# Pair sums and down-projection sums on VectorE instead of GpSimd, in the first and last feed-forward pair and the first down group

## The chip, the core and the metric

The kernel runs on one core of one Trainium2 chip. The metric is the device time of one execution in microseconds (us). Three runs of the kernel before gave 1433.92 to 1436.02 us, with a median of 1434.41 us. The engines are called here as the profile calls them: PE (TensorE matmul), DVE (VectorE), ACT (ScalarE), POOL (GpSimd) and SP (SyncE, whose queue issues the DMAs).

## What is computed

One layer of a decoder, for 1024 tokens of width 1024. The change touches the feed-forward part alone:

```
x = x + concat([y_nsa, y_conv, y_gla]) @ w_out
h = rms_norm(x, ffn_norm_g)
x = x + (silu(h @ ffn_w_gate) * (h @ ffn_w_up)) @ ffn_w_down     # D_FF = 2816
```

All arrays are float32. Ahead of it stand the token mixers and the output projection, behind it a gated per-layer embedding and a last norm.

## The kernel before

**Precision.** Each float32 operand of a product is split in two: `split` (L1037) copies it to the reduced format on ACT (L1039, the high part) and has the rest subtracted on DVE (`sub`, L267, the low part). A product then takes three matmuls: high by high, high by low, low by high. So a matmul waits for ACT where it reads a high part and for DVE where it reads a low part.

**Fewer products.** Gate and up projection run over eleven column groups c of 256. For each c there is one `Pair` for gate (n = 0) and one for up (n = 1). A `Pair` loads two weight tiles `nat` (row blocks m and m+1) and cuts them into four quarters a11, a12, a21, a22. Seven products of quarter sums stand in for eight of quarters (a scheme of the Strassen and Winograd kind). `first` and `second` multiply a11 and a12; `sums` makes s = a21+a22 and then s-a11; `fifth` and `sixth` multiply these; `sixth` also makes a11-a21 and a12-s; `rest` multiplies these and a22, and adds earlier results to later ones (p6+p1, p67+p1). `quarters` puts the four output quarters together and scales them by the norm's factor `rbc1`. For up, the quarters are then multiplied with silu(gate), two of the four (`UPP`) on POOL. On the other side, `Right.make` forms sums of the activations h once (t1 to t4, four tiles each) ahead of the first pair.

In the kernel before, the sums of `Pair.sums`, `sixth` and `rest`, one sum in `quarters`, the two `UPP` products and the sum t3 run on POOL: per c 16 instructions of 128x512 with both inputs in SBUF.

**Down.** The activations of each c go to DRAM (`actd`) as sums; `Down` loads them and two tiles of `w_d` again for groups of up to three c (`DOWN`), and `operands` makes the weight sums: for product 5 b12-b11, for product 6 b22 minus that, for product 7 b22-b12, for product 4 b21 minus the sum. All are on POOL. `drain` adds finished banks into x on DVE (L1335).

**Order.** Two things set it. A dry pass over the code (`_Recorder`) estimates when each tile is last used, with a price per element and engine (`COST`; a `tensor_tensor` on POOL 2.2, on DVE 0.95), and gives each tile one of 50 slots in SBUF; so a tile's load must wait until the tile that had its slot is done. Then the framework puts the instructions of each engine, and the DMAs of SP's queue, in an order by a simulated timeline. Each engine keeps to its order: one that waits holds up all behind it. The last pair (c = 10) and the first down group overlap: `Down` loads and sums stand among the pair's last products.

Of the kernel before, what the change touches and what calls it, by code (L numbers as in the profile page):

```python
# [13 lines left out]
ALU = mybir.AluOpType  # L14
# [12 lines left out]
MF = FF // P  # L27
# [65 lines left out]
UPP = (1, 3)  # L93
PT = 5
PATH = "vvvp"
DOWN = ((0, 1, 2), (3, 4, 5), (6, 7, 8), (9, 10))
# [122 lines left out]
def tile_block(ctx: ExitStack, tc: tile.TileContext, a: dict, out: bass.AP, plan: Plan):  # L219
    nc = tc.nc  # L220
# [27 lines left out]
    class Ring:  # L248


        def __init__(self, lo, hi):
            self.lo, self.hi, self.at = lo, hi, lo
# [13 lines left out]
    def sub(eng, o, i0, i1):  # L266
        return eng.tensor_tensor(out=o, in0=i0, in1=i1, op=ALU.subtract)  # L267
# [449 lines left out]
    for t in range(NT):  # L717
# [11 lines left out]
        if t > 2:  # L729
            pump(near, 1)  # L730
    nc.vector.tensor_tensor(out=gcmp, in0=gates.rearrange("p t (h b) -> p t h b", b=3)[:, :, :, 0],
                            in1=rowok.unsqueeze(2).to_broadcast([P, NT, H]), op=ALU.mult)
# [41 lines left out]
    for which in range(2):  # L774
# [4 lines left out]
        for u in range(2):  # L779
            for g in range(2):  # L780
                src = cv[g * 64:(g + 1) * 64, :].rearrange("p (n j) -> p j n", j=16)
                for q in range(2):
                    js = slice(q * 8, q * 8 + 8)
                    nc.vector.tensor_tensor(
                        out=X[q][u * 64:(u + 1) * 64, :, g * NCMP:(g + 1) * NCMP],
                        in0=src[:, js, u:u + NCMP],
                        in1=pos[g * 64:(g + 1) * 64, u, js].unsqueeze(2).to_broadcast([64, 8, NCMP]), op=ALU.add)
# [249 lines left out]
    def split(src):  # L1037
        o = B("op", F32R, (P, 2, 512))
        nc.scalar.copy(o[:, 0, :], src)  # L1039
        sub(nc.gpsimd if pool_lo[0] > 0 else nc.vector, o[:, 1, :], src, f(o[:, 0, :]))  # L1040
        pool_lo[0] -= 1
        return o

    def half(x, n):
        return x[:, n * 512:(n + 1) * 512]
# [8 lines left out]
    class Right:  # L1054
# [6 lines left out]
        def make(self, *names):  # L1061
            for k, (l, u) in enumerate(zip(self.lower, self.upper)):
                b11, b12 = half(l, 0), half(l, 1)
                b21, b22 = (half(u, 0), half(u, 1)) if u is not None else (None, None)
                for n in names:
                    if n == "t1":
                        sub(nc.vector, b11, b12, b11)
                    if n == "t2":
                        sub(nc.vector, b11, b22, b11)
                    if n == "t3":  # L1070
                        sub(nc.gpsimd, b12, b22, b12)
                    if n == "t4":
                        sub(nc.vector, b11, b21, b11)
                    self.x[n][k] = split({"21": b21, "22": b22, "t3": b12}.get(n, b11))

    class Pair:


        def __init__(self, src, m, right):
            w = []  # L1080
            for i in (m, m + 1):
                w.append(B("nat"))
                nc.sync.dma_start(out=w[-1], in_=src[i])
            self.a11, self.a12, self.a21, self.a22 = (half(w[q // 2], q % 2) for q in range(4))
            self.x, self.b, self.c, self.w5 = right.x, None, None, None

        def first(self, second=True):
            cp = B("cp", F32, (P, 2, 512))
# [10 lines left out]
        def sums(self):  # L1099
            ws = B("ws", F32, (P, 2, 512))  # L1100
            self.s, self.s3 = ws[:, 0, :], ws[:, 1, :]
            nc.gpsimd.tensor_tensor(out=self.s, in0=self.a21, in1=self.a22, op=ALU.add)
            self.w5 = split(self.s)
            sub(nc.gpsimd, self.s, self.s, self.a11)

        def fifth(self):
            if self.w5 is None:
# [7 lines left out]
        def sixth(self):  # L1115
            if self.w5 is None:
                self.sums()
            w6 = split(self.s)
            sub(nc.gpsimd, self.s3, self.a11, self.a21)
            sub(nc.gpsimd, self.s, self.a12, self.s)  # L1120
            self.b = bank()
            prod(w6, self.x["t2"], self.b, True, False)
            nc.scalar.copy(self.p6, self.b)  # L1123

        def rest(self):
            if self.b is None:
                self.sixth()
            s, s3 = self.s, self.s3
            if self.c is None:
                self.fifth()  # L1130
            prod(split(s3), self.x["t3"], self.b, False, False)
            nc.scalar.copy(self.p67, self.b)
            nc.gpsimd.tensor_tensor(out=self.p6, in0=self.p6, in1=self.p1, op=ALU.add)
            nc.gpsimd.tensor_tensor(out=self.p67, in0=self.p67, in1=self.p1, op=ALU.add)
            prod(split(s), self.x["22"], self.c, False, True)
            prod(split(self.a22), self.x["t4"], self.b, False, True)

# [126 lines left out]
    def quarters(p, out):  # L1264

        rr = half(rbc1, 0), half(rbc1, 1)
        add = lambda eng, o, i0, i1: eng.tensor_tensor(out=o, in0=i0, in1=i1, op=ALU.add)
        mult = lambda eng, o, i0, i1: eng.tensor_tensor(out=o, in0=i0, in1=i1, op=ALU.mult)
        c11, c12, c21, c22 = out
        mult(nc.vector, c11, p.a, rr[0])  # L1270
        add(nc.vector, c12, p.c, p.p6)
        mult(nc.vector, c12, c12, rr[1])
        add(nc.vector, c21, p.b, p.p1)
        mult(nc.vector, c21, c21, rr[0])
        add(nc.gpsimd, c22, p.p67, p.p5)
        mult(nc.vector, c22, c22, rr[1])

    for c in range(MF // 2):
        if c == MF // 2 - 1:
            for n in range(2):  # L1280
                pairs[c, n] = Pair(a["w_u" if n else "w_g"], 2 * c, r)
                pairs[c, n].first()
            for n in range(2):
                pairs[c, n].sixth()
            for n in range(2):
                pairs[c, n].fifth()
        for n in range(2):
            if (c, n) not in pairs:
                pairs[c, n] = Pair(a["w_u" if n else "w_g"], 2 * c, r)
                pairs[c, n].first()  # L1290
            p = pairs.pop((c, n))
            p.rest()
            if n == 0:
                act = [B("sg") for _ in range(2)]
                quarters(p, [half(g, i) for g in act for i in range(2)])
                for g in act:
                    nc.scalar.activation(g, g, AF.Silu)
            else:
                up_ = [B("ws", F32, (P, 512)), p.p6, p.p1, p.p5]
                quarters(p, up_)  # L1300
                for i, o in enumerate(up_):
                    g = half(act[i // 2], i % 2)
                    (nc.gpsimd if i in UPP else nc.vector).tensor_tensor(out=g, in0=o, in1=g, op=ALU.mult)

                a11, a21, a12, a22 = (half(g, i) for g in act for i in range(2))
                sa = B("sa", F32, (P, 2, 512))
                s5, s6, s3 = sa[:, 0, :], sa[:, 1, :], up_[0]
                nc.vector.tensor_tensor(out=s5, in0=a21, in1=a22, op=ALU.add)
                sub(nc.vector, s6, s5, a11)
                sub(nc.vector, s3, a12, s6)  # L1310
                sub(nc.vector, a21, a11, a21)
                nc.sync.dma_start(out=actd[c, 0:2].rearrange("i p j -> p i j"), in_=sa)
                nc.sync.dma_start(out=actd[c, 2], in_=s3)
                nc.sync.dma_start(out=actd[c, 3:5].rearrange("i p j -> p i j"), in_=act[0].rearrange("p (i j) -> p i j", i=2))
                nc.sync.dma_start(out=actd[c, 5], in_=a22)
                nc.sync.dma_start(out=actd[c, 6], in_=a12)
# [17 lines left out]
    def add(o, i0, eng=nc.vector):  # L1334
        eng.tensor_tensor(out=o, in0=i0, in1=o, op=ALU.add)  # L1335

    class Down:


        def __init__(self, c):  # L1340
            self.c, self.a = c, {}
            w = []
            for m in (2 * c, 2 * c + 1):
                w.append(B("nat"))
                nc.sync.dma_start(out=w[-1], in_=a["w_d"][m * P:(m + 1) * P, :])
            self.b11, self.b12, self.b21, self.b22 = (half(x, i) for x in w for i in range(2))
            self.load(5, 6)
            st = B("st", F32, (P, 2, 512))
            self.t, self.a[2] = st[:, 0, :], st[:, 1, :]
            nc.sync.dma_start(out=self.a[2], in_=actd[c, 6])  # L1350
# [7 lines left out]
        def operands(self, n):  # L1358
            x = self
            if n == 5:  # L1360
                x.load(3, 1)
                sub(nc.gpsimd, x.t, x.b12, x.b11)
            if n == 6:
                sub(nc.gpsimd, x.t, x.b22, x.t)
            if n == 3:
                x.load(7, 4)
            if n == 7:
                sub(nc.gpsimd, x.b12, x.b22, x.b12)
            if n == 4:
                sub(nc.gpsimd, x.t, x.b21, x.t)  # L1370
            return split(x.a.pop(n)), split({3: x.b22, 1: x.b11, 7: x.b12, 2: x.b21}.get(n, x.t))
# [30 lines left out]
    for q, cs in enumerate(DOWN):  # L1402
        ds = [Down(c) for c in cs]
        for n, g, start in ((5, 0, True), (6, 1, True), (3, 0, False), (1, 0, True), (7, 1, False), (4, 1, False),
# [17 lines left out]
            for t in range(4):  # L1422
                c = slice(t * P, (t + 1) * P)
# [26 lines left out]
    for i, t in enumerate(ORDER):  # L1450
        c = slice(t * P, (t + 1) * P)
        x, r3 = rows[i]
# [128 lines left out]
```

## Time and profile before

| | |
|---|---|
| median of three runs | 1434.41 us (1433.92 to 1436.02) |
| profiled execution | 1426.49 us, of which its span 1424.7 us |
| PE busy | 1380.7 us, 97% |
| DVE busy | 1034.4 us, 73% |
| POOL busy | 692.8 us, 49% |
| ACT busy | 662.6 us, 47% |
| mean granted PE clock | 0.993 |

The profile is of one execution, so durations and waits are read from it and set against its 1426.49 us. A stretch is given in us from the start of the span. The output projection ends at 636 us, the feed-forward pairs fill 636 to about 1081 us, and the first down group begins at 1076 us among the last pair's products. A PE row in brackets tells how long PE stood idle before an instruction and what ended the wait. POOL spans are rough.

### The profile page before, as it was taken

The numbers are of one execution on the slowest core, as the hardware profiler recorded it, in microseconds if no ns is written. First come the engines' busy times: TensorE is split into PE (matmuls) and PEld (weight loads), VectorE is DVE, ScalarE is ACT, GpSimd is POOL, SyncE is SP. The second block draws the span as 40 slices with busy tenths as digits, with TensorE's granted clock in tenths as the row PEclk, the third lists the DMA queues.
The fourth block names the chain that finished last, engine by engine and source line by source line (L and its number), as shares of the span: only waits on it lengthen the run. The fifth ranks groups of instructions, "written<-read, shape, count | busy, mean of one in ns | idle before, by whom it ended". The sixth has DMA issues, their size and how long they took to land.

```text
span 1424.7 us, 19476 instructions
## 1 busy us (share of the span) xinstructions
PE 1380.7 (97%) x7080; PEld 1159.6 (81%) x7080; DVE 1034.4 (73%) x1782; ACT 662.6 (47%) x1290; POOL 692.8 (49%) x680
## 2 busy tenths in 40 slices
PE   8999999999999989999899999999998999999997
PEld 6898777889999978887788877877786878887886
DVE  3897548468999885658767767676788998887533
ACT  7321522257888884545433333333334444444532
POOL 3751433438887872045566555655485514303111
PEclk9999999999999999999999999999999999999999
DMA  9201012500000023521232331233365733521111
GB/s 361 68 16 40 25 53 86 167 1 5 9 5 5 5 79 119 188 79 45 100 109 95 110 108 63 83 110 111 141 235 205 258 132 127 171 81 63 68 41 45
DMA packets 55743, 135.68 MB, mean 95 GB/s; under 512 B 5412, under 2 KB 10206, under 8 KB 55646
## 3 DMA queue, kind: packets, MB, share of 16 engines
q1 hardware_dynamic: 55502, 134.42, 27.1%
q8 instruction: 55, 0.90, 0.3%
q14 instruction: 42, 0.34, 0.1%
q10 hardware_dynamic: 144, 0.01, 0.0%
HBM read 102.68 MB, written 31.73 MB: 94 GB/s over the span
## 4 chain that ended last, share of the span: by engine, by line
PE 58%; DVE 16%; POOL 9%; ACT 6%; issue 6%; DMA 4%; SPq 0%; POOLq 0%; DVEq 0%; ACTq 0%
DVE op L267 8%; PE banks L1426 7%; POOL ws L267 4%; PE banks L966 3%; PE banks L371 3%; PE banks L372 3%; PE banks L368 3%; ACT op L1039 3%; PE banks L1010 2%; PE banks L1011 2%; PE banks L906 2%; PE banks L1476 2%; PE banks L1477 2%; PE banks L1478 2%; PE banks L907 2%
## 5 line engine op out<-in xcount | busy, mean ns | idle before, releaser
L1050 PE MATMUL banks<-op 128*128 128x512 f32 x616 | 238.8, 394 | 4.7 <-ACT cp L1123 3.0
L1052 PE MATMUL banks<-op 128*128 128x512 f32 x616 | 239.8, 392 | 3.0 <-DVE op L267 3.0
L1051 PE MATMUL banks<-op 128*128 128x512 f32 x616 | 240.7, 391 | 0.7 <-DVE op L267 0.7
L1426 PE MATMUL banks<-op 128*128 128x512 f32 x924 | 214.8, 394 | 8.4 <-DVE op L267 4.6
L1426 PEld LDWEIGHTS banks<-op 128*128 128x128 f32 x924 | 174.8, 190 | 48.0 <-DVE op L267 6.5
L1039 ACT CAST op<-nat 128x512 fp32r<-128x512 f32 x200 | 117.7, 619 | 174.3 <-DVE op L267 64.0
L267 DVE TENSOR_TENSOR op<-nat,op 128x512 fp32r<-128x512 f32 x196 | 164.9, 864 | 38.5 <-ACT op L1039 37.9
L267 DVE TENSOR_TENSOR op<-ws,op 128x512 fp32r<-128x512 f32 x88 | 99.5, 1131 | 73.4 <-ACT op L1039 69.6
L1050 PEld LDWEIGHTS banks<-op 128*128 128x128 f32 x616 | 115.9, 188 | 36.6 <-ACT cp L1123 8.9
L1052 PEld LDWEIGHTS banks<-op 128*128 128x128 f32 x616 | 116.0, 188 | 28.8 <-DVE op L267 3.9
L1051 PEld LDWEIGHTS banks<-op 128*128 128x128 f32 x616 | 116.1, 188 | 24.7 <-DVE op L267 1.1
L921 POOL TENSOR_SCALAR p<-p,sums,gates 128x640 f32<-128x640 f32 (+7 forms) x128 | 100.4, 795 | 36.4 <-DVE sums L917 26.8
L1039 ACT CAST op<-ws 128x512 fp32r<-128x512 f32 x88 | 54.0, 623 | 105.1 <-POOL ws L267 65.1
L912 ACT ACTIVATE p<-p,mn 128x640 f32<-128x640 f32 (+7 forms) x128 | 94.7, 742 | 10.2 <-DVE mn L909 10.1
L368 PE MATMUL banks<-hT,whi 128*128 128x512 f32 x208 | 83.9, 404 | 6.8 <-ACT hT L324 6.3
L371 PE MATMUL banks<-hT,whi 128*128 128x512 f32 x208 | 83.4, 401 | 0.5 <-DVE hT L325 0.5
L372 PE MATMUL banks<-hT,wlo 128*128 128x512 f32 x208 | 82.1, 396 | 0.0
L966 PE MATMUL banks<-cst,p 128*128 128x128 f32 x448 | 71.2, 274 | 2.3 <-DVE pt L267 1.3
L906 PE MATMUL banks<-k,qst 128*128 128x512 f32 (+2 forms) x192 | 68.0, 360 | 1.0 <-POOL qst L267 0.5
L267 DVE TENSOR_TENSOR pt<-banks,pt 128x512 fp32r<-128x512 f32 (+1 forms) x114 | 64.1, 570 | 6.1 <-ACT pt L977 5.2
L1335 DVE TENSOR_TENSOR x<-banks,x 128x512 f32<-128x512 f32 x96 | 63.4, 679 | 5.5 <-PE banks L1426 5.4
L267 POOL TENSOR_TENSOR st<-nat 128x512 f32<-128x512 f32 x11 | 21.1, 1919 | 90.7 <-DMA nat<-in_w_d 84.2
(299 smaller groups left out, 3402.0 us busy)
## 6 DMA issues: line engine op xcount, KB each, us to landing
nat<-actd SPq DMA_DIRECT2D x33, 512.0 KB, 5.6
nat<-in_w_g SPq DMA_DIRECT2D x22, 512.0 KB, 3.2
nat<-in_w_u SPq DMA_DIRECT2D x22, 512.0 KB, 4.0
nat<-in_w_d SPq DMA_DIRECT2D x22, 512.0 KB, 6.2
nat<-in_w_t SPq DMA_DIRECT2D x13, 512.0 KB, 4.2
actd<-sg SPq DMA_DIRECT2D x22, 256.0 KB, 2.2
actd<-sa SPq DMA_DIRECT2D x11, 512.0 KB, 5.3
actd<-sg SPq DMA_DIRECT2D x11, 512.0 KB, 5.3
```

What stands on the lines that cost most here:

```text
L267: return eng.tensor_tensor(out=o, in0=i0, in1=i1, op=ALU.subtract)
L368: r = mm(o, hi[:, w], x[:, 0, :], start=kt == 0, stop=False)
L371: mm(o, hi[:, w], x[:, 1, :], start=False, stop=False)
L372: mm(o, lo_[:, w], x[:, 0, :], start=False, stop=kt == KT - 1)
L906: mark("pe", mm(ps[:, :max(w, 256)], q, kdup[br][g][:, k], start=True, stop=False))
L921: nc.gpsimd.tensor_scalar(out=ps_out[br][:, :n], in0=ps_out[br][:, :n], scalar1=sums[:, br:br + 1], scalar2=gates[:, qb, 3 * head(h) + 1 + ...
L966: nc.tensor.transpose(ps[:, (2 * m + e) * P:(2 * m + e + 1) * P], blk(e, kb, br, ka), ident)
L1039: nc.scalar.copy(o[:, 0, :], src)
L1050: mm(ps, w[:, 0, c], x[k][:, 0, :], start=start and k == 0, stop=False, skip_group_check=True)
L1051: mm(ps, w[:, 0, c], x[k][:, 1, :], start=False, stop=False, skip_group_check=True)
L1052: mm(ps, w[:, 1, c], x[k][:, 0, :], start=False, stop=k == 3, skip_group_check=True)
L1426: mm(groups[g][t], r[:, v, c], l[:, u, :], start=start and (i, u, v) == (0, 0, 0), stop=i == len(ops) - 1 and u == 1, skip_group_check=True)
```

## The change

`Pair` and `Down` get an attribute `eng`. It is DVE for the pairs of c = 0 and c = 10 (m = 0 and MF-2) and for the down products of the first group (c = 0, 1, 2), and POOL elsewhere. The sums named above use it; of `Down.operands`, those for products 5 and 6, while those for 7 and 4 stay on POOL. The four sums t3 go to DVE too. Per `Pair` that is seven instructions, for up two more: 4 x 7 + 2 x 2 = 32, with t3 36, with 3 x 2 of `Down` 42 instructions, all 128x512 float32 with both inputs in SBUF.

```
                     if n == "t3":
-                        sub(nc.gpsimd, b12, b22, b12)
+                        sub(nc.vector, b12, b22, b12)
...
             self.x, self.b, self.c, self.w5 = right.x, None, None, None
+
+            self.eng = nc.vector if m in (0, MF - 2) else nc.gpsimd
...
-            nc.gpsimd.tensor_tensor(out=self.s, in0=self.a21, in1=self.a22, op=ALU.add)
+            self.eng.tensor_tensor(out=self.s, in0=self.a21, in1=self.a22, op=ALU.add)
             self.w5 = split(self.s)
-            sub(nc.gpsimd, self.s, self.s, self.a11)
+            sub(self.eng, self.s, self.s, self.a11)
...
-            sub(nc.gpsimd, self.s3, self.a11, self.a21)
-            sub(nc.gpsimd, self.s, self.a12, self.s)
+            sub(self.eng, self.s3, self.a11, self.a21)
+            sub(self.eng, self.s, self.a12, self.s)
...
-            nc.gpsimd.tensor_tensor(out=self.p6, in0=self.p6, in1=self.p1, op=ALU.add)
-            nc.gpsimd.tensor_tensor(out=self.p67, in0=self.p67, in1=self.p1, op=ALU.add)
+            self.eng.tensor_tensor(out=self.p6, in0=self.p6, in1=self.p1, op=ALU.add)
+            self.eng.tensor_tensor(out=self.p67, in0=self.p67, in1=self.p1, op=ALU.add)
...
-        add(nc.gpsimd, c22, p.p67, p.p5)
+        add(p.eng, c22, p.p67, p.p5)
...
-                    (nc.gpsimd if i in UPP else nc.vector).tensor_tensor(out=g, in0=o, in1=g, op=ALU.mult)
+                    (p.eng if i in UPP else nc.vector).tensor_tensor(out=g, in0=o, in1=g, op=ALU.mult)
...
             self.c, self.a = c, {}
+            self.eng = nc.vector if c in DOWN[0] else nc.gpsimd
...
-                sub(nc.gpsimd, x.t, x.b12, x.b11)
+                sub(x.eng, x.t, x.b12, x.b11)
...
-                sub(nc.gpsimd, x.t, x.b22, x.t)
+                sub(x.eng, x.t, x.b22, x.t)
```

The order of the engines' instructions moves with it. Three places matter here.

First SP's queue at the second column group. `nat_6896` and `nat_6898` are the first and second weight tile of its up pair (c = 1, n = 1); the `sg` and `sa` rows are stores of the first column group's activations. Before:

```order
L1083 DMA nat_6763<-in_w_g 128x1024
L1083 DMA nat_6765<-in_w_g 128x1024
L1083 DMA nat_6898<-in_w_u 128x1024
L1315 DMA actd_2366<-sg_6665 128x512
L1083 DMA nat_6896<-in_w_u 128x1024
L1312 DMA actd_2366<-sa_6753 128x2x512
```

The same place of the changed kernel:

```order
L1083 DMA nat_6763<-in_w_g 128x1024
L1083 DMA nat_6765<-in_w_g 128x1024
L1083 DMA nat_6896<-in_w_u 128x1024
L1317 DMA actd_2366<-sg_6665 128x512
L1318 DMA actd_2366<-sg_6665 128x512
L1083 DMA nat_6898<-in_w_u 128x1024
L1314 DMA actd_2366<-sa_6753 128x2x512
```

The first tile stood behind a store and now stands ahead of it; the second stands behind two stores.

Next DVE where the last pair (`ws_9352`, `cp_9260`, `cp_9296`) meets the first down group (`st_9539` and `st_9547` are weight sums, the `op` rows low parts). Before:

```order
L1268 TENSOR_TENSOR ws_9511<-banks_67,rbc1_6583 128x512
L267 TENSOR_TENSOR op_9358<-ws_9352,op_9358 128x512
L267 TENSOR_TENSOR op_9563<-st_9539,op_9563 128x512
L267 TENSOR_TENSOR op_9481<-ws_9352,op_9481 128x512
L267 TENSOR_TENSOR op_9560<-nat_9537,op_9560 128x512
L267 TENSOR_TENSOR op_9496<-nat_9294,op_9496 128x512
L267 TENSOR_TENSOR op_9572<-st_9547,op_9572 128x512
```

Of the changed kernel:

```order
L1270 TENSOR_TENSOR ws_9511<-banks_67,rbc1_6583 128x512
L267 TENSOR_TENSOR st_9539<-nat_9533 128x512
L1270 TENSOR_TENSOR sg_9452<-banks_67,rbc1_6583 128x512
L267 TENSOR_TENSOR op_9358<-ws_9352,op_9358 128x512
L1135 TENSOR_TENSOR cp_9260<-cp_9260 128x512
L267 TENSOR_TENSOR ws_9352<-nat_9292,ws_9352 128x512
L267 TENSOR_TENSOR op_9563<-st_9539,op_9563 128x512
L267 TENSOR_TENSOR op_9560<-nat_9537,op_9560 128x512
L267 TENSOR_TENSOR st_9539<-nat_9535,st_9539 128x512
L267 TENSOR_TENSOR op_9481<-ws_9352,op_9481 128x512
L267 TENSOR_TENSOR op_9496<-nat_9294,op_9496 128x512
L267 TENSOR_TENSOR st_9547<-nat_9541 128x512
```

The sums now stand among the low parts; three of them read weight tiles of the down group (`nat_9533`, `nat_9535`, `nat_9541`) that SP's queue loads at this place.

Last POOL at the same place. Before:

```order
L267 TENSOR_TENSOR st_9547<-nat_9541 128x512
L267 TENSOR_TENSOR nat_9541<-nat_9543,nat_9541 128x512
L1133 TENSOR_TENSOR cp_9296<-cp_9296 128x512
L267 TENSOR_TENSOR st_9547<-nat_9543,st_9547 128x512
L1134 TENSOR_TENSOR cp_9376<-cp_9376,cp_9260 128x512
L1267 TENSOR_TENSOR sg_9453<-cp_9376 128x512
L267 TENSOR_TENSOR st_9555<-nat_9549 128x512
```

Of the changed kernel:

```order
L267 TENSOR_TENSOR nat_9533<-nat_9535,nat_9533 128x512
L267 TENSOR_TENSOR nat_9541<-nat_9543,nat_9541 128x512
L267 TENSOR_TENSOR nat_9549<-nat_9551,nat_9549 128x512
L267 TENSOR_TENSOR st_9539<-nat_9535,st_9539 128x512
L267 TENSOR_TENSOR st_9547<-nat_9543,st_9547 128x512
L267 TENSOR_TENSOR st_9555<-nat_9551,st_9555 128x512
```

Only the six sums for products 7 and 4 are left on POOL there.

## Rows read from the trace of the kernel before

**Rows 1.** The page's part 1: busy us, share of span, instructions.

```profile
PE 1380.7 (97%) x7080; PEld 1159.6 (81%) x7080; DVE 1034.4 (73%) x1782; ACT 662.6 (47%) x1290; POOL 692.8 (49%) x680
```

**Rows 2.** Seven stretches: length, busy us (instructions) of PE, PEld, DVE, ACT, POOL, PE clock, DMA.

```profile
625.00:664.00 39.00, 38.30 (x177) 31.45 (x176) 35.48 (x43) 24.49 (x42) 19.48 (x16) 1.00 0.11 41
664.00:700.00 36.00, 31.23 (x126) 24.02 (x125) 28.00 (x30) 13.28 (x22) 28.06 (x25) 0.96 0.27 95
690.00:700.00 10.00, 5.91 (x19) 4.12 (x18) 7.93 (x9) 2.73 (x5) 6.08 (x4) 0.85 0.54 202
1050.00:1092.00 42.00, 36.18 (x150) 27.92 (x148) 35.24 (x32) 18.70 (x34) 36.08 (x23) 0.97 0.84 298
1100.00:1112.00 12.00, 12.00 (x55) 9.94 (x54) 12.00 (x21) 6.79 (x13) 0.00 (x0) 1.00 0.76 271
1090.00:1100.00 10.00, 9.31 (x30) 6.96 (x29) 10.00 (x16) 4.46 (x8) 2.49 (x2) 0.68 0.08 13
...
1180.00:1220.00 40.00, 40.00 (x178) 33.14 (x177) 36.22 (x54) 19.51 (x34) 12.57 (x8) 1.00 0.22 76
```

**Rows 3.** PE in order of time: start, us, instruction, [idle before, releaser].

```profile
650.63 0.50 PE L1051 MATMUL banks<-op 128*128 128x512 f32 x1 [0.70 <-DVE op L267]
...
667.88 1.13 PE L342 MATMUL banks<-dg 128*128 128x512 f32 x2 [0.68 <-POOL dg L339]
...
692.62 0.50 PE L1050 MATMUL banks<-op 128*128 128x512 f32 x1 [1.36 <-ACT op L1039]
...
696.09 0.50 PE L1052 MATMUL banks<-op 128*128 128x512 f32 x1 [2.73 <-DVE op L267]
...
1075.85 0.50 PE L1426 MATMUL banks<-op 128*128 128x512 f32 x1 [0.83 <-ACT op L1039]
...
1077.51 1.33 PE L1426 MATMUL banks<-op 128*128 128x512 f32 x3 [1.15 <-DVE op L267]
...
1089.15 2.20 PE L1426 MATMUL banks<-op 128*128 128x512 f32 x5 [2.81 <-DVE op L267]
1092.04 28.16 PE L1426 MATMUL banks<-op 128*128 128x512 f32 x114 [0.69 <-DVE op L267]
...
1145.63 14.56 PE L1426 MATMUL banks<-op 128*128 128x512 f32 x63 [2.32 <-DVE x L1335]
```

**Rows 4.** SP's queue in order of time, at the second column group's up pair.

```profile
680.41 0.33 SPq L1083 DMA_DIRECT2D nat<-in_w_u  x1
688.08 0.33 SPq L1315 DMA_DIRECT2D actd<-sg  x1
688.52 0.36 SPq L1083 DMA_DIRECT2D nat<-in_w_u  x1
```

**Rows 5.** ACT in order of time, at the same pair.

```profile
691.95 1.14 ACT L1039 CAST op<-nat 128x512 fp32r<-128x512 f32 x2 [4.40 <-DMA nat<-in_w_u]
```

**Rows 6.** POOL in order of time, at the three waits named.

```profile
684.61 3.44 POOL L1303 TENSOR_TENSOR sg<-cp,sg 128x512 f32<-128x512 f32 x2
...
1073.33 1.29 POOL L267 TENSOR_TENSOR st<-nat 128x512 f32<-128x512 f32 x1
...
1085.15 3.40 POOL L1303 TENSOR_TENSOR sg<-cp,sg 128x512 f32<-128x512 f32 x2
```

**Rows 7.** DVE in order of time: low parts with POOL idle, and beside it.

```profile
652.84 1.88 DVE L267 TENSOR_TENSOR op<-raw,op 128x512 fp32r<-128x512 f32 x3
...
694.29 2.35 DVE L267 TENSOR_TENSOR op<-nat,op 128x512 fp32r<-128x512 f32 x2
...
1053.84 1.77 DVE L267 TENSOR_TENSOR op<-ws,op 128x512 fp32r<-128x512 f32 x1
```

**Rows 8.** Groups by line, shapes apart: busy us, mean ns of one | idle before, releaser.

```profile
L267 DVE TENSOR_TENSOR op<-ws,op 128x512 fp32r<-128x512 f32 x88 | 99.5, 1131 | 73.4 <-ACT op L1039 69.6
...
L1335 DVE TENSOR_TENSOR x<-banks,x 128x512 f32<-128x512 f32 x96 | 63.4, 679 | 5.5 <-PE banks L1426 5.4
```

**Rows 9.** One line's instructions: minimum, median, maximum ns, first and last start.

```profile
L1102 POOL TENSOR_TENSOR ws<-nat x22: 1277/1292/1750, 625.8 to 1049.8; 128x512 f32<-128x512 f32 x22
```

## Prediction

> **What bounds the kernel now.** I read the page's part 1 first: PE is busy for 97% of the span [rows 1], so a change is worth what it does to PE's idle time and to PE's clock, and nothing else. The next view is PE in order of time, for its idle times in the two places that the change touches [rows 3], and then the busy time of each engine in stretches around these [rows 2].
>
> At full pace PE issues 178 matmuls in 40 us, 0.225 us each [rows 2]. At the start of the feed-forward part it idles 0.70, 0.68, 1.36 and 2.73 us, together 5.47 us [rows 3]. The last two stand in the stretch 690 to 700, where 19 matmuls were issued and 10 / 0.225 = 44.5 would fit: 25.5 x 0.225 = 5.7 us lost, of which 4.1 are idle. The other 1.6 us are the clock, granted at 0.85 on average there, so part of the stretch ran at the lower of its two levels after the idle time [rows 2]. **The start loses 7.1 us.** Where the last pair meets the first down group, PE idles 0.83, 1.15, 2.81 and 0.69 us, together 5.48 us [rows 3]; from 1090 to 1100 it issued 30 matmuls at a mean clock of 0.68, so 14.5 x 0.225 = 3.3 us are lost, 0.7 of them idle, and 2.6 are the clock. **The end loses 8.1 us**, and 2.32 us more at 1145 where PE waits for DVE to empty a bank [rows 3]. All of it is 17.5 us; no gain from this change can be much larger.
>
> What ends these waits: at 692 ACT casts a weight tile that has just landed [rows 5]. Its load was issued at 688.52, right behind a store at 688.08 [rows 4], and that store waited for the second of two POOL products, 684.61 to 688.05 [rows 6]. The load itself was free to go long before. At 1075 the last weight sum comes from POOL at 1073.33, and at 1089 POOL has just spent 3.40 us on two products [rows 6]. Most others are low parts from DVE, which is slow for a reason that lies on POOL as well.
>
> **What an instruction costs on either engine.** On POOL a sum takes 1.29 us, up to 1.75 [rows 9]. On DVE the same shape takes 0.68 us where one input is in PSUM [rows 8], and three in a row with POOL idle take 1.88 us, so one follows another after (1.88 - 0.68) / 2 = 0.60 us [rows 7]. With both inputs in SBUF and POOL busy, one takes 1.77 us, 1.1 more [rows 7]; over all 88 low parts of this kind the mean is 1.13 us [rows 8]. So each POOL sum delays a waiting DVE by about 1.1 us, and moving it to DVE costs 0.60 us. Where DVE is the late engine, the move relieves it.
>
> The Trainium skill (SBUF — State Buffer, section "Who interferes with whom") says that a VectorE instruction with two SBUF inputs and a GpSimd instruction that reads SBUF share an interface, and that the second to issue waits until the first is finished. The 1.77 us agrees in kind; a full wait behind 1.29 us would be a little more than the 1.1 seen. By that rule the sums below would have 1.3 in place of 1.1, which takes about 2.6 us off the gain.
>
> **The change part by part.** 42 instructions go from POOL to DVE: at the start 2 of t3 before 625, and then 11 from 625 to 664 and 7 from 664 to 700; at the end 4 before 1050 and 18 from 1050 to 1092. POOL's 16, 25 and 23 instructions in these three stretches [rows 2] are these 11, 7 and 18, the sums that stay (0, 8 and 5), and 5 and 10 small ones for the norm's factor.
>
> *625 to 664.* DVE is busy 35.5 us with 43 instructions [rows 2]. With the moved ones it has 54 at 0.60, 32.4 us, and POOL is left with two fills and a few small ones that form the norm's factor, which no longer stand behind sums. The 0.70 us (a low part late on DVE) and the 0.68 us (POOL's factor late) go.
>
> *664 to 700.* DVE has 30 instructions in 28.0 us [rows 2]; 37 at 0.60 are 22.2, and the eight sums of the second column group that stay on POOL add up to 8 x 1.1 = 8.8, together 31.0. SP's queue changes with it: the pair's first tile is loaded ahead of the stores. Its slot was last used by a22 of the up pair before, whose product ends, counted back 33 matmuls in the new PE order, 7.5 us ahead of the need. The load before took 3.4 us from issue to the cast (688.52 to 691.95) and the cast is the first of two in 1.14 us [rows 4, 5], together some 4 to 5 us. So it is in time by about 2.5 us, and 1.36 + 2.73 + 1.6 us go. The second tile now stands behind two stores that wait for DVE; it is needed some ten us after the first, which covers it. The stretch shrinks from 36 to 36 - 0.68 - 5.7 = 29.6 us, and DVE's 31.0 don't quite fit: I take off 1.4. **Start: 7.1 - 1.4 = 5.7 us.**
>
> *1050 to 1092.* Here lies the main question. DVE has 32 instructions in 35.2 us, 1.10 each, while POOL is busy for 36.1 of 42 us [rows 2]. Afterwards DVE has 50 at 0.60, 30.0 us, and the five sums left on POOL add up to 5.5: 35.5 us, as before, for 18 instructions more, and no result goes to POOL and back on the way to PE. The stretch shrinks to 42 - 8.1 = 33.9 us, and 35.5 doesn't fit by 1.6. **End: 8.1 - 1.6 = 6.5 us.** Bounds: a moved instruction can cost nothing net, which gives all 8.1, or DVE keeps its 1.10 us each (the next part).
>
> *1145.* From 1090 to 1100 and from 1100 to 1112 DVE is busy all the time, though POOL does little or nothing there [rows 2]; the second group's sums stay on POOL. DVE gets there earlier by about as much as PE does. I take half of the 2.32: **1.2 us.**
>
> *Between the two places* the same work runs in nearly the same order. Loads change places in a few column groups; the cover is a pair's 20 us of matmuls. I count nothing, within 1.5 us to either side.
>
> Sum: 5.7 + 6.5 + 1.2 = 13.4 us, from 1426.5 to 1413.1 us in the profiled execution. The three runs have a median 7.9 us above it; I take the same gain there: 1434.4 - 13.4 = **1421.0 us**.
>
> **The rivals.** *VectorE becomes the bound.* DVE has no free time from 1090 to 1112 [rows 2], and 22 instructions are put right ahead. If its 1.10 us are not POOL's doing but the operands' (both inputs in SBUF, in any company), 50 instructions take 55 us where 42 are there: 13 us longer, less the 5.7 of the start: 1434.4 + 13 - 5.7 = 1441.7 us. It decides where an instruction takes over 42 / 50 = 0.84 us. For it speaks the mean of 1.13 over 88 [rows 8]; against it the three at 0.60 with SBUF inputs while POOL was idle, and 21 in 12 us while POOL did nothing [rows 7, 2]. Chance 0.10. The Trainium skill (Perfetto Trace Analysis, section "Optimizing Scalar/DVE Operations") advises to move work off a saturated VectorE, to GpSimd among others, which is this rival's direction; it adds that the two share a read port, so that moving work between them might not help.
>
> *DVE waits for loads.* Three sums of the first down group were POOL's to wait for. DVE keeps its order, and behind a sum whose tile is late stand low parts of the last pair that PE needs. Each us late beyond a slack of some 2 us goes to PE. DMA is 84% busy in that stretch [rows 2], so 3 to 8 us are possible; the end's 7.7 us would be lost, or a little less: 1426 to 1434, most likely 1429. Against it: POOL's sum of the third tile started at 1073.33, late because POOL was, not for a load [rows 6]. Chance 0.10, 0.04 of it faster.
>
> *One place pays, the other doesn't*, say the load is late at the start, or a low part is late on DVE some 20 us into the down group: a gain of 6 to 8 us, 1427 us. Chance 0.18.
>
> *Nothing moves:* PE's idle time goes elsewhere, 1434. Chance 0.06.
>
> **How the numbers follow.** The forecast has 0.56 (1416 to 1425 by itself; 1416.9 is all 17.5 us). A measurement of this kernel tells 0.2%, 2.9 us, from no change. Faster by more than that: 0.56 + 0.18 + 0.04 = 0.78. The same: 0.06 + 0.06 = 0.12. Slower: 0.10. From 1416 to 1432 lie the forecast, the third rival and about half of the second, near 0.8.
>
> **What would show it.** Right: no idle time of over 1 us on PE from 640 to 700, a load of the first tile (nat<-in_w_u) ahead of the first store of sg there, PE's clock at 1.00 from 690 to 700 and near 1.00 at the end; DVE's mean at the end under 0.75 us, with some 50 instructions there. Wrong: low parts of 1.1 us with POOL idle (first rival), DVE idle before a sum st<-nat with a DMA as its releaser (second rival), a wait of PE near 1090 to 1100 of 3 us or more. If the profile loses 5 to 8 us at one place only, the other's step is at fault.

## The result, and the profile after

The changed kernel takes 1414.04 us (median of four executions, 1412.33 to 1414.87). The kernel before, with one execution more, takes 1434.16 us (1431.32 to 1436.02). The ratio is 0.988 with a 95% interval of 0.9859 to 0.9901: **20.1 us faster, where 13.4 were forecast**, and 2 us below the low end of the stated range. The two profiled executions differ by 1426.49 - 1413.34 = 13.2 us, almost exactly the sum of the forecast. So there are two questions: were the terms right in the profile, and why do the medians lie 7 us further apart than the profiles?

The page's part 1 of the changed kernel, to be read against [rows 1]. POOL has 42 instructions and 64 us less. DVE has 42 more and is busy for only 4.6 us more.

```profile
PE 1375.8 (97%) x7080; PEld 1159.2 (82%) x7080; DVE 1039.0 (74%) x1824; ACT 663.6 (47%) x1290; POOL 628.9 (45%) x638
```

Stretches of the changed kernel, with the columns of [rows 2]. The work of 1050 to 1092 in the kernel before is now done some 6 us earlier, so 1044 to 1086 stands for it.

```profile
625.00:664.00 39.00, 39.00 (x182) 32.54 (x181) 35.73 (x58) 25.43 (x43) 5.73 (x9) 1.00 0.11 41
664.00:700.00 36.00, 36.00 (x157) 29.06 (x156) 28.66 (x39) 16.25 (x26) 16.41 (x15) 1.00 0.31 110
690.00:700.00 10.00, 10.00 (x46) 8.29 (x45) 7.65 (x10) 5.09 (x9) 7.58 (x5) 1.00 0.52 188
...
720.00:1040.00 320.00, 314.72 (x1371) 255.60 (x1370) 236.33 (x269) 114.97 (x195) 183.49 (x127) 1.00 0.29 102
...
1044.00:1086.00 42.00, 42.00 (x187) 34.77 (x186) 40.34 (x59) 21.17 (x37) 11.94 (x6) 1.00 0.81 290
...
1104.00:1109.00 5.00, 2.77 (x10) 1.96 (x9) 5.00 (x10) 0.00 (x0) 4.20 (x3) 0.87 0.99 357
1109.00:1114.00 5.00, 5.00 (x20) 3.98 (x19) 4.87 (x7) 1.64 (x3) 4.84 (x4) 0.79 0.62 237
```

From 625 to 700, PE has no idle time left at all, at a clock of 1.00 throughout. From 1044 to 1086 it has none either, and DVE does 59 instructions in 40.34 us there, 0.68 each, where it did 32 at 1.10 before [rows 2]. The low parts op<-ws show it over the whole span (columns of [rows 8], where their mean was 1131 ns):

```profile
L267 DVE TENSOR_TENSOR op<-ws,op 128x512 fp32r<-128x512 f32 x88 | 92.7, 1058 | 56.7 <-ACT op L1039 51.4 <-PE banks L1052 2.0
```

The waits of PE that matter now, in order of time (columns of [rows 3]): one at 730 that is new, and three where the first down group runs. Counted by the down projection's matmuls, the wait of 2.32 us at 1145 in the kernel before [rows 3] stood ahead of the 253rd. That matmul now starts at 1132.81, and around it (last row) PE has no idle time. The 2.23 us at 1106 stand ahead of the 145th, where the kernel before didn't wait.

```profile
729.94 0.50 PE L1050 MATMUL banks<-op 128*128 128x512 f32 x1 [1.73 <-ACT op L1039]
...
1089.39 3.70 PE L1429 MATMUL banks<-op 128*128 128x512 f32 x15 [0.79 <-DVE x L1337]
1093.59 10.74 PE L1429 MATMUL banks<-op 128*128 128x512 f32 x46 [0.50 <-DVE op L267]
1106.57 3.71 PE L1429 MATMUL banks<-op 128*128 128x512 f32 x10 [2.23 <-DVE x L1337]
```

```profile
1120.00:1140.00 20.00, 20.00 (x90) 16.57 (x89) 18.97 (x27) 8.48 (x15) 7.26 (x5) 1.00 0.24 80
```

SP's queue at the second column group (as [rows 4]), and, after the dots, at the third:

```profile
680.41 0.33 SPq L1083 DMA_DIRECT2D nat<-in_w_u  x1
684.31 0.33 SPq L1317 DMA_DIRECT2D actd<-sg  x1
...
687.09 0.43 SPq L1083 DMA_DIRECT2D nat<-in_w_u  x1
...
725.18 0.33 SPq L1317 DMA_DIRECT2D actd<-sg  x1
725.61 0.36 SPq L1083 DMA_DIRECT2D nat<-in_w_u  x1
```

ACT's casts of these tiles, and its copy behind the seventh product of the tenth group's up pair:

```profile
684.31 0.62 ACT L1039 CAST op<-nat 128x512 fp32r<-128x512 f32 x1
...
729.27 1.14 ACT L1039 CAST op<-nat 128x512 fp32r<-128x512 f32 x2 [6.91 <-DMA nat<-in_w_u]
...
1026.31 0.59 ACT L1134 COPY cp<-banks 128x512 f32<-128x512 f32 x1 [1.94 <-PE banks L1052]
```

The first tile is issued at 680.41, ahead of the store, and ACT casts it at 684.31 without a wait; before, it was issued at 688.52 and cast at 691.95 [rows 4, 5]. One column group later the old pattern stands again. A load (725.61) follows a store (725.18) that waits for a POOL product, ACT waits 6.91 us for the tile, and PE waits 1.73 us for ACT. The stall was not only taken away: a part of it moved to the next group.

**Where the 13.2 us came from.** The same copy of ACT in the kernel before:

```profile
1032.28 0.59 ACT L1132 COPY cp<-banks 128x512 f32<-128x512 f32 x1 [2.08 <-PE banks L1052]
```

So 5.97 us are gained by there. The matmuls on `cst` of the last part, of before and of after, are 12.92 us apart:

```profile
1310.77 0.60 PE L1443 MATMUL banks<-cst,x 128*128 128x128 f32 x4
```

```profile
1297.85 0.60 PE L1446 MATMUL banks<-cst,x 128*128 128x128 f32 x4
```

The start and the stretch behind it gave 6.0 us, the end 12.92 - 5.97 = 6.95. By PE's state, from the spans and part 1 of the two pages: its idle time went from 1424.7 - 1380.7 = 44.0 to 1411.5 - 1375.8 = 35.7 us, 8.3 less, and its busy time, for the same 7080 matmuls, fell by 4.9 us. Most of that is clock: the mean went from 0.993 to 0.995, and 0.002 x 1425 is 2.9 us.

### The profile page after: what moved, and what is told of

The parts are those of the page before. It is cut to its first block, busy times and chain, and to the rows that moved or that the text cites. A ratio compares the mean times of both kernels' runs of the same rounds, so it can differ in the third digit from the quotient of the medians.

```text
span 1411.5 us, 19461 instructions
## 1 busy us (share of the span) xinstructions
PE 1375.8 (97%) x7080; PEld 1159.2 (82%) x7080; DVE 1039.0 (74%) x1824; ACT 663.6 (47%) x1290; POOL 628.9 (45%) x638
## 4 chain that ended last, share of the span: by engine, by line
PE 71%; DVE 12%; POOL 5%; issue 4%; ACT 4%; DMA 3%; SPq 0%; POOLq 0%; DVEq 0%; ACTq 0%
PE banks L1429 9%; DVE op L267 5%; PE banks L1050 5%; PE banks L1052 5%; PE banks L1051 5%; PE banks L966 3%; PE banks L371 3%; PE banks L372 3%; PE banks L368 3%; PE banks L1010 2%; PE banks L1011 2%; PE banks L906 2%; PE banks L1151 2%; PE banks L1152 2%; PE banks L1479 2%
## 5 line engine op out<-in xcount | busy, mean ns | idle before, releaser
L267 DVE TENSOR_TENSOR op<-nat,op 128x512 fp32r<-128x512 f32 x196 | 160.6, 845 | 36.4 <-ACT op L1039 35.5
L267 DVE TENSOR_TENSOR op<-ws,op 128x512 fp32r<-128x512 f32 x88 | 92.7, 1058 | 56.7 <-ACT op L1039 51.4
L437 DVE SCALAR_TENSOR_TENSOR banks<-glu,par,banks 128x1023 f32<-128x1023 f32 (+24 forms) x50 | 63.7, 1275 | 1.7
```

## The experiments

All runs are set against executions of the kernel before that ran beside them on the same chip: medians of 1431.69 us (first four kernels), 1431.25 (next four), 1430.61 (last four).

**The whole again, and each place alone.** The changed kernel was run as it is, and then with `eng` on VectorE for one place only:

```
start only:  self.eng = nc.vector if m == 0 else nc.gpsimd        # Down: nc.gpsimd; t3 on VectorE
end only:    self.eng = nc.vector if m == MF - 2 else nc.gpsimd   # Down as changed; t3 on GpSimd
```

> The changed kernel again, beside new runs of the kernel before. In the profiled executions it is 13.2 us shorter (1426.49 against 1413.34), in the medians 20.1 us (1434.16 against 1414.04). Theory A: the change is worth what PE no longer loses in the profile, some 13 us, and the rest is drift between runs: then the medians now differ by 12 to 15 us. Theory B: in most executions the waits of the kernel before are longer than in the one profiled, and the change takes these away too: then the medians differ by 18 to 22 us again, and executions of the kernel before spread wider (1426 to 1436) than those of the changed one (1412 to 1415).

> Only the start: the sums of the first pair and t3 go to VectorE; the last pair and the down products stay on GpSimd. By the profiles the changed kernel has lost 7.0 us less than the kernel before by 720 us, and gives 1.2 back by 900. Theory A: 5 to 7 us faster than before in the median. Theory B, if the 7 us by which the medians exceed the profile belong to the late load at the start: 12 to 14 us faster. If they belong to the end: 5 to 7 us.

> Only the end: the sums of the last pair and of products 5 and 6 of the first down group go to VectorE; the first pair and t3 stay on GpSimd. The forecast gave 6.5 us to the end and 1.2 to the wait at 1145; by the profiles it is 7.4 us from 1010 us on. Theory A: 6 to 8 us faster in the median, and start and end add up to the whole change within 2 us. Theory B, if what the medians have above the profile belongs to the end: 13 to 15 us. The rival that VectorE becomes the bound: no gain or slower.

The whole took 1413.47 us (ratio 0.988, 0.9861 to 0.9898), 18.2 us faster. That is the difference of theory B, but not its narrow spread (1412.48 to 1418.95 us), and longer waits as its cause are not shown by this (see the section on the medians below). The start alone took 1424.04 (0.9943, 0.9931 to 0.9955), 7.7 us faster, and the end alone 1423.11 (0.9939, 0.9927 to 0.9952), 8.6 us faster. Both places pay, each some 1 to 2 us more than its term. Their sum of 16.3 us is 2 us short of the whole, which is within the intervals.

**The start: the engine or the place of the load?** The first run has the two products with silu(gate) of the first group on VectorE and nothing else; the second is the whole change with these two back on GpSimd.

```
-  (nc.gpsimd if i in UPP else nc.vector).tensor_tensor(...)
+  (nc.vector if c == 0 else nc.gpsimd if i in UPP else nc.vector).tensor_tensor(...)    # these two alone
+  ((nc.gpsimd if c == 0 else p.eng) if i in UPP else nc.vector).tensor_tensor(...)      # changed kernel, two back
```

> Of the whole change two instructions alone: the two products of up with silu(gate) of the first column group go to VectorE, all sums stay on GpSimd. In the order of SP's queue the first tile of the second up pair now stands behind more stores than before, not ahead of them. If the start's loss hangs on how late GpSimd finishes these two products, 3 to 5 us are gained; if it hangs on the place of the load in SP's queue, as the forecast says, the wait at 690 to 696 us stays and the time is within 2 us of before, or some us slower.

> The changed kernel with the two products of up with silu(gate) of the first column group back on GpSimd. In SP's queue both tiles of the second up pair now stand ahead of all stores. If the place of the load is what counts at the start, there is no wait at 690 to 700 us and the time is within 2 us of the changed kernel (1413 to 1416). If the engine of these products counts, 3 to 6 us of wait come back: 1417 to 1420.

The two alone take 1431.05 us (0.9992, 0.998 to 1.0004), no difference. SP's queue, and then PE, of that run:

```profile
690.28 0.33 SPq L1317 DMA_DIRECT2D actd<-sg  x1
692.21 0.38 SPq L1314 DMA_DIRECT2D actd<-sa  x1
692.70 0.40 SPq L1083 DMA_DIRECT2D nat<-in_w_u  x1
```

```profile
698.39 0.80 PE L1050 MATMUL banks<-op 128*128 128x512 f32 x1 [3.48 <-ACT op L1039]
```

The load now stands behind two stores, and PE waits 3.48 us for the cast. With the two back on GpSimd it is 1414.69 us (0.9884, 0.9865 to 0.9904), the same as the changed kernel. SP issues both tiles ahead of the stores, and PE waits 0.41 us:

```profile
680.29 1.91 SPq L1083 DMA_DIRECT2D nat<-in_w_u  x2
```

```profile
692.80 0.50 PE L1052 MATMUL banks<-op 128*128 128x512 f32 x1 [0.41 <-DVE op L267]
```

So the waits at 692 and 696 were not a matter of who computes the two products. They go with the load's place in the queue, as the prediction had it. No run moved the load alone: its place always changed together with where some of the sums are computed.

**The end: which sums?** One run has the last pair's 16 alone on VectorE (`Down` on GpSimd), another the six of the first down group alone (all pairs on GpSimd).

> Of the end only the last pair's 16 sums go to VectorE; those of the first down group, the first pair and t3 stay on GpSimd. If the moved sums count by what they cost VectorE (some 0.9 us beside each on GpSimd, by the run with the additional sums, against 0.60 on VectorE itself) and by GpSimd's results coming earlier, most of the end's 8.6 us are here: 5 to 8 us faster than before. If the lateness of the down group's sums on GpSimd is what counts: 0 to 3 us.

> Of the end only the six sums for products 5 and 6 of the first down group go to VectorE. If the last pair's sums carry the end: 1 to 3 us faster than before. If the down group's sums do: 5 to 8 us.

The last pair alone gives 1422.87 us (0.9941, 0.9927 to 0.9955), 7.7 us faster, nearly the whole end. The six alone give 1431.89 us (1.0009, 0.9996 to 1.0022), no difference. With these six on VectorE the 0.83 us at 1075 [rows 3] are gone, but for the rest PE waits where it waited before, and longer at the last place, 3.45 us for 2.32:

```profile
1078.57 0.74 PE L1429 MATMUL banks<-op 128*128 128x512 f32 x2 [1.19 <-DVE op L267]
...
1089.09 3.47 PE L1429 MATMUL banks<-op 128*128 128x512 f32 x14 [1.45 <-DVE op L267]
1094.39 9.15 PE L1429 MATMUL banks<-op 128*128 128x512 f32 x39 [1.84 <-DVE cp L1269]
...
1147.51 12.76 PE L1429 MATMUL banks<-op 128*128 128x512 f32 x48 [3.45 <-DVE x L1337]
```

So POOL's late weight sum at 1073.33 [rows 6] was not what held PE up by itself. With 16 sums of the last pair still on POOL, DVE was as late without it. That it is POOL's sums that slow DVE down is what the next two runs test.

**What a sum on GpSimd costs VectorE.** One run is the changed kernel with the six sums for products 7 and 4 of the first down group on VectorE too. The other is the same with 22 additional sums on GpSimd, whose results nobody reads.

```
-                sub(nc.gpsimd, x.b12, x.b22, x.b12)
+                sub(x.eng, x.b12, x.b22, x.b12)
-                sub(nc.gpsimd, x.t, x.b21, x.t)
+                sub(x.eng, x.t, x.b21, x.t)
...
+    def twin(on, o):            # behind each moved sum of the last pair and of products 5 and 6; o is its result
+        if on:
...
+            nc.gpsimd.tensor_tensor(out=dmy[0], in0=o, in1=dmy[0], op=ALU.add)
```

> The changed kernel, and the six sums of the first down group that it left on GpSimd (for products 7 and 4) on VectorE as well. Each costs VectorE 0.60 us and takes away a GpSimd sum that, by the forecast, costs a waiting VectorE 1.1: VectorE gains 6 x 0.5 = 3 us around 1050 to 1080, and the waits behind it at 1089, 1093 and 1106 (0.79, 0.50 and 2.23 us, with the clock after them) shrink: 2 to 4 us faster than the changed kernel, 1409 to 1412. The rival, that VectorE is full and each sum on it costs its own time: 2 to 4 us slower, 1416 to 1418.

> The same kernel with 22 additional sums on GpSimd, one beside each sum of the last pair and of products 5 and 6 that went to VectorE; each reads that sum's result and adds it to a tile that nobody reads, so nobody waits for a GpSimd sum there. If GpSimd's sums slow VectorE down by 1.1 us each, the end takes some 15 to 24 us more: 1425 to 1435 us, with low parts of 1.7 us and more on VectorE from 1045 to 1100. If what the change removed was only the lateness of GpSimd's results, the time stays within 2 us of the kernel without the additional sums.

Six more take 1414.46 us (0.9882, 0.9863 to 0.9901), so the median shows neither the 2 to 4 us gained nor the rival's loss. The profile shows more. The wait of 2.23 us at 1106 is down to 0.67:

```profile
1109.12 1.21 PE L1429 MATMUL banks<-op 128*128 128x512 f32 x4 [0.67 <-DVE x L1337]
```

But PE has lost time ahead of 588 us, where all these kernels do the same work. These are the first 588 us of the changed kernel and of this one:

```profile
0.00:588.00 588.00, 569.65 (x3497) 497.97 (x3498) 422.43 (x1006) 319.76 (x706) 317.35 (x400) 0.99 0.20 68
```

```profile
0.00:588.00 588.00, 569.61 (x3475) 497.77 (x3476) 420.13 (x1003) 316.31 (x702) 316.35 (x400) 0.99 0.20 65
```

PE is busy as long and has done 22 matmuls fewer, 5.0 us at 0.225 each. The granted clock is 0.83 from 160 to 170 us and 0.89 from 290 to 305 and from 450 to 465 us, where the changed kernel has 1.00 in all three. The whole profile is only 2.2 us longer (1413.7 - 1411.5), so from 588 us on it is some 2.8 us shorter, as expected. Why the median doesn't show these stays open.

With the 22 additional sums it is 1434.52 us (1.0024, 1.0013 to 1.0036), **20.1 us more** than without them. Windows of the two, first without:

```profile
1045.00:1100.00 55.00, 54.52 (x241) 44.83 (x240) 53.90 (x90) 30.38 (x52) 0.00 (x0) 1.00 0.83 296
```

```profile
1045.00:1100.00 55.00, 41.93 (x161) 31.28 (x159) 54.76 (x64) 22.66 (x39) 27.88 (x18) 0.91 0.75 266
```

DVE is busy all the time in both. With POOL idle it does 90 instructions, 53.90 / 90 = 0.60 us each. With 18 sums on POOL it does 64, which at 0.60 are 38.3 us; the other 16.4 us are 16.4 / 18 = 0.91 us for each sum on POOL. The time of the kernel gives the same figure, 20.1 / 22 = 0.91, though PE's clock has a part in it (0.91 in this stretch, against 1.00 without these sums). The low parts of that run in this stretch, by group:

```profile
L267 DVE TENSOR_TENSOR op<-ws,op 128x512 fp32r<-128x512 f32 x5 | 6.5, 1338 | 0.0
```

The prediction's 1.1 us, read from one pair of rows [rows 7], was 0.2 us too high. The direction is settled: the profile shows no instruction that waits for one of these sums, and they undo the whole gain.

The Trainium skill (SBUF — State Buffer, section "Who interferes with whom") states that a VectorE instruction with two SBUF inputs contends with a GpSimd instruction that reads SBUF. The run agrees; a full wait behind each sum, at 1.29 us, would have been 28 us and not 20.1.

**Why the medians differ more than the profiles.** The kernel before was run once more for a second profile.

> The kernel before once more, for a second profiled execution. The first took 1426.49 us, less than any of the 20 other executions (1428.83 to 1436.02). If the distance is in PE's clock, this one is near 1431 us with the same waits to a few tenths (5.5 us of idle time between 640 and 700, 5.8 between 1050 and 1100, 2.3 to 2.6 at 1145), and with a lower granted clock behind one or two of them, where the first profile had 1.00, as the profile of the two products alone had behind 698 and 1150 us. If it is in the waits, some of these are longer by 2 us or more, or the span grows ahead of 560 us.

It took 1428.91 us, with a span of 1427.1, 2.4 us more than in the first profile. PE's idle time is the same, 1427.1 - 1383.5 = 43.6 us against 44.0; its busy time for the same matmuls is 2.8 us longer. Most of that is the clock behind the wait at 1145. The first profile (wait of 2.32 us [rows 3]):

```profile
1145.00:1150.00 5.00, 4.37 (x19) 3.65 (x20) 5.00 (x9) 0.88 (x2) 0.00 (x0) 1.00 0.06 19
1150.00:1155.00 5.00, 5.00 (x23) 4.14 (x23) 5.00 (x9) 3.19 (x7) 0.00 (x0) 1.00 0.00 0
```

The second, PE and the same stretches:

```profile
1146.72 13.47 PE L1426 MATMUL banks<-op 128*128 128x512 f32 x51 [2.59 <-DVE x L1335]
```

```profile
1145.00:1150.00 5.00, 3.28 (x11) 2.60 (x12) 5.00 (x9) 0.66 (x2) 0.00 (x0) 0.81 0.21 80
1150.00:1155.00 5.00, 5.00 (x20) 4.08 (x19) 4.59 (x9) 1.83 (x3) 0.00 (x0) 0.85 0.01 2
```

The wait is 0.27 us longer, and the clock behind it is 0.81 and 0.85 in place of 1.00, which costs 0.19 x 5 + 0.15 x 5 = 1.7 us. The kernel with the two products alone, which differs from the one before in little, shows more of it. Its profiled execution has a span of 1431.9 us, 7.2 longer. PE is idle for 43.2 us of it, no more than before, and busy for 1388.7, 8.0 more; its mean clock is 0.988 against 0.993, and 0.005 x 1430 = 7.2. Two of the places follow. The first lies ahead of 588 us, where nothing was changed; the kernel before has a clock of 1.00 there and 85 matmuls. By 588 us this run is 16 matmuls behind it (3485 against 3501), 3.6 us, so half of the 7.2 us have nothing to do with the two places of this change.

```profile
290.00:305.00 15.00, 15.00 (x72) 12.79 (x71) 6.29 (x24) 5.80 (x18) 4.61 (x7) 0.77 0.00 0
...
1150.00:1155.00 5.00, 4.26 (x12) 3.38 (x13) 5.00 (x9) 0.78 (x2) 0.00 (x0) 0.66 0.05 14
```

In all 49 executions of the kernel before with a clock on record, the time goes with it:

| mean granted clock | executions | mean time, us |
|---|---|---|
| 0.988 and 0.989 | 14 | 1433.2 |
| 0.990 and 0.991 | 17 | 1431.2 |
| 0.992 to 0.994 | 18 | 1429.2 |

The first profile, at 0.993 and 1426.49 us, is the second fastest of them. The changed kernel's nine have a median of 0.995, as its profile has. Where in the kernel an execution without a profile lost its clock is not on record. Of the 14 profiles, 6 show a lower clock in at least one of the three stretches named above ahead of 588 us; both profiles of the kernel before and both of the changed one have 1.00 there.

**Further on the same way.** The first run has all these sums, in all groups, on VectorE. The second puts the two kernels above with less idle time into one: the first group's two products back on GpSimd, and the six more sums on VectorE.

> All of these sums go to VectorE, in all eleven column groups and all four down groups. If a sum costs VectorE 0.60 us and one on GpSimd 0.9 to 1.1, VectorE is as busy as before or less, the late loads of the next groups (a wait of 1.7 us at 730 behind a store that waits for GpSimd) and the other waits between 720 and 1050 (4.9 us in all) mostly go, and the low parts have a mean near 0.70 us: 2 to 5 us faster than the changed kernel, 1409 to 1412. The rival, that VectorE becomes the bound (in the middle 20 more instructions in 50 us in which it is busy for 36): 1416 to 1430.

> The changed kernel with the first group's two products with silu(gate) back on GpSimd, which puts both loads of the second up pair ahead of the stores, and with the six sums of the first down group for products 7 and 4 on VectorE. By their profiles each of the two has some 2 us less idle time on PE than the changed kernel: 1410 to 1413 together, if PE's clock doesn't take it back; 1413 to 1415 if it does.

All on VectorE take 1417.38 us (0.9904, 0.9885 to 0.9923), 13.2 us faster than before but 3 to 4 behind the changed kernel. The expected gain isn't there. Two stretches of it:

```profile
720.00:1040.00 320.00, 314.54 (x1374) 256.61 (x1373) 241.60 (x389) 113.58 (x191) 0.00 (x0) 1.00 0.30 103
...
1100.00:1105.00 5.00, 1.86 (x6) 1.25 (x7) 5.00 (x10) 3.32 (x6) 0.00 (x0) 0.89 1.01 349
```

In the middle DVE does 120 instructions more than in the changed kernel for 5.3 us more (241.60 against 236.33), and PE is busy as long (314.54 against 314.72): even. There one instruction takes 241.60 / 389 = 0.62 us with POOL idle, so each of POOL's 127 instructions in the changed kernel cost (236.33 - 269 x 0.62) / 127 = 0.55 us of DVE, about as much as it saves (an estimate, which takes 0.62 us for DVE's own instructions in both). At 1100 DVE is full, sums of the second down group stand among its low parts, and PE does 6 matmuls in 5 us. That is the first rival's mechanism, VectorE as the bound, at one place and one step beyond this change. It is not all of the loss: of the 5.6 us that this profile is longer than the changed kernel's (1417.1 - 1411.5), 13 matmuls or 2.9 us lie ahead of 588 us (3484 against 3497), at a clock of 0.77 from 290 to 305. How the 3 to 4 us of the medians divide is not shown. The Trainium skill (Perfetto Trace Analysis, section "Optimizing Scalar/DVE Operations") says that moving work between these two engines might not help; in this middle it does not, while at the two places of the change it did.

The mix takes 1411.16 us (0.9861, 0.9847 to 0.9874), **19.5 us faster than before**. Its four executions (1410.69 to 1411.62) all lie below the nine of the changed kernel (1412.33 to 1418.95), so it is the fastest seen. The lead of 2 to 3 us is about as much as a measurement can tell, and the intervals of the two ratios overlap. There is no wait of over 0.4 us near 730, and the waits in the first down group are small, the largest of them:

```profile
1103.58 16.61 PE L1429 MATMUL banks<-op 128*128 128x512 f32 x72 [0.69 <-DVE x L1337]
1129.46 30.88 PE L1429 MATMUL banks<-op 128*128 128x512 f32 x135 [1.10 <-ACT op L1039]
```

## Why the prediction was right, and where it was not

- *What bounds the kernel.* This was right: PE's idle time and clock, at the two places named.
- *Start, 5.7 us.* In the profile PE has no idle time from 625 to 700 and did 339 matmuls there, 36 more than before (303 [rows 2]), or 8.1 us at 0.225 each. So at least the 7.1 us went; the 1.4 us taken off for DVE were not needed (28.66 us busy, not 31.0). The mechanism, the load ahead of the store, agrees with the two runs on it.
- *Between, 0 within 1.5 us.* This term was mis-sized. From 720 to 1040 PE idles 320 - 314.72 = 5.28 us and before 3.38 (row below), so 1.9 us came back, nearly all in the wait at 730. The cover of a pair's matmuls that the step counted on did not hold where a load again stands behind a waiting store. With the start it makes 6.0 gained, for 5.7. That the two agree so well is luck: one term was some 2 us too small and the other 1.9 us too large.

```profile
720.00:1040.00 320.00, 316.62 (x1376) 256.58 (x1376) 228.02 (x260) 114.68 (x193) 185.37 (x131) 1.00 0.29 103
```

- *End, 6.5, and 1145, 1.2 us.* Together they came to 6.95 for 7.7. DVE did fit (59 instructions at 0.68 where some 50 below 0.75 were expected). The sum hides two errors. The 2.32 us at 1145 went whole and not by half. In their place PE waits 2.23 us at 1106, 108 matmuls earlier, for a drain that DVE does behind a run of low parts, and the clock of 0.87 and 0.79 there was to be near 1.00.
- *Price of a sum on GpSimd for VectorE.* The step assumed 1.1 us; 0.91 was measured where DVE is full and 0.55 estimated in the middle. The 0.60 on DVE itself holds.
- *The step that failed* is the last of the sum: "I take the same gain there", from the profiled execution to the median, and with it the ceiling of 17.5 us. It assumed that the 7.9 us between the two are a constant. Part of them are PE's clock: behind a wait like that at 1145 it falls in some executions and not in others, and the change takes most of these waits away. That this is where the executions without a profile lose it is not shown, since the clock also fell where the kernels are the same. In the second comparison the gain is 18.2 us, 5.0 more than in the profiles. The second profiles of the two kernels are 14.3 us apart (1427.1 - 1412.8), so the agreement of 13.2 with 13.4 is in part luck too. The median clock is 0.991 before and 0.995 after, the profiles' are 0.993 and 0.995; the 0.002 by which before's differ are 2 to 3 us. The other 2 to 3 us, and why three executions of the first comparison, without a clock on record, lie some 3 us higher still (1433.92 to 1436.02), stay open.
- *Rivals.* VectorE did not become the bound; with all sums on it, it did at one place. No sum of the down group waited long for a load. Both places paid.

## What to carry to other kernels

Before a gain in a profile is carried over to the median, take a second profile of the same kernel: the two profiles of one kernel here were 2.4 us apart, most of it clock, and the median execution lay 4 to 5 us above the first (1430.61 to 1431.69 against 1426.49). Compare the two profiles also ahead of the first changed instruction, since what differs there is not the change's doing. When work moves between VectorE and GpSimd, count what a GpSimd instruction takes from VectorE (0.55 to 0.91 us for 1.29 here) against what it costs there (0.60): at a place where VectorE is the late engine it pays, in the middle it is even, and where VectorE is full already it is lost. And look at each queue for loads behind stores that wait for arithmetic; a change of the order can move such a stall to the next group.

## What the runs showed that was not expected

- Executions of one kernel without any other difference spread over 8.6 us (1426.36 to 1434.92), in step with a granted clock of 0.994 to 0.988.
- A wait of about 2.2 to 2.3 us can go either way. In the kernel before (2.32 us at 1145) and in the second profile of the changed kernel (2.21 us at 1107.88) the clock stayed at 1.00; in the first profile of the changed kernel (2.23 us) it fell. After the waits of 2.59 and 2.60 us ahead of the same matmul as the one at 1145, seen in three profiles, it fell each time.
- The clock also fell where nothing was changed. In the profile of the kernel with six more sums on VectorE PE is idle for 1413.7 - 1380.3 = 33.4 us, 2.3 less than in the changed kernel, and busy for 4.5 more. The 5.0 us lost ahead of 588 us are more than that. From 720 to 740 both kernels are busy for 18.0 us, at a clock of 0.92 there and of 1.00 in the changed kernel, and at 1109 it is the changed kernel that loses clock.
